# A linear recurrence's gate products: three rounded passes in place of plain fp32, in a planned one-core decoder kernel

## The chip, the cores and the metric

The kernel runs on one core of one Trainium2 chip. The metric is the device time of one execution in microseconds (us). Before the change three runs gave 982.98, 983.00 and 983.11 us, a median of 983.0.

## The reference, cut to what matters

One layer of a hybrid decoder: 512 tokens, model width 1024. Three token mixers read one input projection; their outputs are projected, multiplied by sigmoid gates, summed and projected again; cross-attention and a gated feed-forward network follow. The change lies in the first mixer, a gated linear recurrence over 512 channels in 4 blocks of 128:

```python
def rg_lru(u, w_a, b_a, w_i, b_i, lam):          # u: 512 tokens x 512 channels, after a causal conv
    ub = u.reshape(B_, L, LRU_BLOCKS, LRU_BLOCK)
    r = jax.nn.sigmoid(jnp.einsum('blhi,hij->blhj', ub, w_a).reshape(B_, L, BRANCH_W) + b_a)
    i = jax.nn.sigmoid(jnp.einsum('blhi,hij->blhj', ub, w_i).reshape(B_, L, BRANCH_W) + b_i)
    log_a = -LRU_C * r * jax.nn.softplus(-lam)
    a = jnp.exp(log_a)
    mult = jnp.sqrt(-jnp.expm1(2.0 * log_a))
    _, h = lax.associative_scan(_linear_combine, (a, mult * (i * u)), axis=1)
    return h
...
    y_a = rg_lru(causal_dwconv(u_lru, conv_w, conv_b), ...) * jax.nn.gelu(g_lru)
...
    merged = jnp.sum(gates * jnp.einsum('blnw,nwd->blnd', ys, w_branch), axis=2)
    return merged @ w_mix_out
```

The two einsums with `w_a` and `w_i` are the gate products: for each of 4 blocks and 2 kinds one product of a 128 x 128 weight and a 128 x 512 activation. The second mixer (GLA) is a chunked gated linear attention on q, k, v with a normalised output times silu(og). The third (S5) is a complex diagonal state-space model.

## The kernel before, in words

Activations lie with channels on 128 partitions and 512 tokens along the free axis, so most tiles are 128 x 512 floats. Almost every large product is done by `mm3`: both operands are split into a rounded high part (type fp32r, by a ScalarE Copy) and the rest (by a VectorE subtract), and three fp32r matmuls add high x high, high x low and low x high into one PSUM tile. The split of a weight is named `whi<-raw` (ScalarE, 128 x 1024) and `wlo<-raw,whi` (VectorE, 128 x 1024); that of a 128 x 512 activation is made by `hilo` (high part on ScalarE, low part on VectorE). The gate products `lg` of the recurrence are an exception: they are eight plain fp32 matmuls.

TensorE's stream has a foreground, written out in a fixed order: the projections us, u, g, qk (four tiles each), lr, v and og (tile `vo`), then for 24 output tiles a gate projection `gt` (24 matmuls) and a branch product `br` (12 matmuls), whose product with the gate is added up. The first eight `br` tiles read branch A, that is the recurrence's output `ya`, the next eight branch B (`yb`, GLA), the last eight branch C. Around it run background generators: `lru()` (the recurrence), `gla()` and the S5 routines. They are woven in by a planner. Each engine is wrapped by a class that adds up a guessed time for each instruction issued to it; at each `slot()` in the foreground a background generator may go on as long as VectorE and ScalarE are guessed to be less than a lead ahead of TensorE, and as long as what it waits for is guessed to be ready. The planner's guess for a matmul of n columns is n/2.4 + 13 ns in fp32r and n/0.6 + 26 ns in plain fp32. The guesses only set the order in which each engine's instructions are written; on the chip each engine runs its own list in that order, and waits at an instruction whose input or memory is not there.

Two pools of memory matter. All 128 x 512 SBUF tiles come from one heap of `NHEAP = 52` slots; a tile that is allocated into a slot may be written only when the last reader of the slot's earlier tile is through. PSUM tiles likewise take the slots of earlier PSUM tiles.

Names that are used below:

- `uc` is the conv's output, `lg` the gate products, `lgs` their sigmoids. `ea` and `th` come from an exponential and a tanh of them; three VectorE operations make a and 1-a^2 out of them; four ScalarE square roots (`ea<-ea`) give the factor of the input; then per block one VectorE product (`lgs<-lgs,ea`) and one VectorE scan (`ea<-th,lgs`), then the product with the GeLU gate (`ea<-ea,g`) and the split into `ya` high (ScalarE) and low (VectorE).
- In `gla()`: `keT` (transposes and copies), `dS` (state increments, 56 matmuls in two halves), `Sp` (14 VectorE steps that run the state over chunks), `att`, `o`, then for each of four token tiles `ob`: four ScalarE squares that sum into `ms`, a POOL power, four VectorE products; at the end `ybT`, transposes of the four `ob`.
- In S5: `Et` (transposes) and `G` (products), `E`, `C`, `tm` (VectorE products for tables), `es`, `esw`, `vv`, `zs` (its scan), `Xs`, `y`.
- `vo` on VectorE adds a bias, and on ScalarE is the silu of og. `th<-gt` and `th<-th,br` finish a gate and multiply it by its branch tile.

In the profile almost every instruction carries line 75 (the wrapper's `return f(*a, **k)`), so rows are told apart by tile names.

Of the kernel before, what the change touches and what calls it, by code (L numbers as in the profile page):

```python
# [16 lines left out]
P = 128  # L17
# [141 lines left out]
def hybrid_kernel(ctx: ExitStack, tc: tile.TileContext, I, out, dbg=None):  # L159
# [17 lines left out]
    def H(s, dt=F32):  # L177
        t = heap.tile([P, 512], dt, tag="h", name=nm(s))
        plan.life[t.name] = [plan.seq, plan.seq, nslot[0]]
        return t  # L180
# [10 lines left out]
    def PS(s):  # L191
        return psp.tile([P, 512], F32, tag="ps", name=nm(s))
# [3 lines left out]
    T, SP = Engine(nc.tensor, pe_cost, plan), Engine(nc.sync, sp_cost, plan)  # L196

    def split(hi, lo, src):
        A.activation(hi, src, AF.Copy)
        V.tensor_tensor(lo, src, hi.bitcast(F32), ALU.subtract)  # L200

    def hilo(s, src):
        hi, lo = H(s, F32R), H(s, F32R)
        split(hi, lo, src)
        return hi, lo

    def tap(name, ap, idx=None):
        if dbg is not None and name in dbg:
            d = dbg[name] if idx is None else dbg[name][idx]
            SP.dma_start(d, ap)  # L210
# [157 lines left out]
    def hold(n):  # L368

        while held[0] + n > NHOLD and not rush[0]:  # L370
            yield -1
        held[0] += n
# [31 lines left out]
    def note(x):  # L404
        LOG.append((nslot[0], x))
# [34 lines left out]
    def mm3(ps, w, x, first, last, **k):  # L440
        T.matmul(ps, lhsT=w[0], rhs=x[0], start=first, stop=False, **k)
        T.matmul(ps, lhsT=w[0], rhs=x[1], start=False, stop=False, **k)
        T.matmul(ps, lhsT=w[1], rhs=x[0], start=False, stop=last, **k)

    def cut(pair, *idx):
        return pair[0][idx], pair[1][idx]

    ALL = slice(None)
# [27 lines left out]
    def col(name, i=0, n=1):  # L476
        c = COLS[name] + i
        return pc[:, c:c + n]
# [108 lines left out]
    for f in range(8):  # L587
# [3 lines left out]
        o = ps[:, (f % 2) * 256:(f % 2) * 256 + 256]  # L591
# [28 lines left out]
    def lru_sp():  # L620
        lam = col("lam", 0, 4)
        t0, t1, t2, z, z2, acc = (S("sp", 4) for _ in range(6))
        V.tensor_scalar(t0, lam, -1.0, None, ALU.mult)
        V.tensor_tensor(t1, lam, t0, ALU.max)
        A.activation(t1, t1, AF.Exp, scale=-1.0)
        V.tensor_scalar(t2, t1, 2.0, None, ALU.add)
        V.reciprocal(t2, t2)
        V.tensor_tensor(z, t1, t2, ALU.mult)
        V.tensor_tensor(z2, z, z, ALU.mult)
        V.memset(acc, 1.0 / 17.0)  # L630
        for n in (15, 13, 11, 9, 7, 5, 3, 1):
            V.tensor_tensor(acc, acc, z2, ALU.mult)
            V.tensor_scalar(acc, acc, 1.0 / n, None, ALU.add)
        V.tensor_tensor(acc, acc, z, ALU.mult)
        V.tensor_scalar(t0, t0, 0.0, None, ALU.max)
        V.scalar_tensor_tensor(t0, acc, 2.0, t0, ALU.mult, ALU.add)
        V.tensor_scalar(lrsp[:, 0:4], t0, -8.0, None, ALU.mult)
        V.tensor_scalar(lrsp[:, 4:8], t0, 4.0, None, ALU.mult)
        yield 0
# [3 lines left out]

    def lru():
        yield from lru_sp()
        uc = []
        wa = [H("wa"), H("wi")]
        SP.dma_start(wa[0], I["lru_wa"])
        SP.dma_start(wa[1], I["lru_wi"])
        for b in range(4):  # L650
            o = H("uc")
            V.tensor_scalar(o, ug[b], col("cw", 12 + b), col("cb", b), ALU.mult, ALU.add)
            yield 0
            for s in range(1, 4):
                V.scalar_tensor_tensor(o[:, s:], ug[b][:, :SEQ - s], col("cw", 4 * (3 - s) + b), o[:, s:],
                                       ALU.mult, ALU.add)
                yield 0
            uc.append(o)
        ug.clear()
        yield T, uc[0], wa[0], wa[1]  # L660
        r, iu = [], []
        for b in range(4):
            yield from hold(2)
            pss = [PS("lg"), PS("lg")]
            for kind in range(2):
                T.matmul(pss[kind], lhsT=wa[kind][:, b * P:(b + 1) * P], rhs=uc[b], start=True, stop=True)
            yield A, pss[0], pss[1]
            for kind in range(2):
                o = H("lgs")
                A.activation(o, pss[kind], AF.Sigmoid, bias=col("bi" if kind else "ba", b))  # L670
                (iu if kind else r).append(o)
            held[0] -= 2
            yield 0
        for b in range(4):
            V.tensor_tensor(iu[b], iu[b], uc[b], ALU.mult)
        uc.clear()
        yield 0
        a, m = [], []
        for b in range(4):
            ea, th = H("ea"), H("th")  # L680
            A.activation(ea, r[b], AF.Exp, scale=lrsp[:, b:b + 1])
            A.activation(th, r[b], AF.Tanh, scale=lrsp[:, 4 + b:5 + b])
            yield V, ea, th
            V.scalar_tensor_tensor(th, ea, 1.0, th, ALU.add, ALU.mult)
            V.scalar_tensor_tensor(ea, th, 2.0, th, ALU.subtract, ALU.mult)
            V.tensor_scalar(th, th, -1.0, 1.0, ALU.mult, ALU.add)
            a.append(th)
            m.append(ea)
            yield 0
        r.clear()  # L690
        for b in range(4):
            A.activation(m[b], m[b], AF.Sqrt, scale=-1.0)
        lru_done.append(True)
        for b in range(4):
            yield V, m[b]
            V.tensor_tensor(iu[b], iu[b], m[b], ALU.mult)
            V.tensor_tensor_scan(m[b], a[b], iu[b], 0.0, ALU.mult, ALU.add)
            tap("lru_h", m[b], b)
            yield 0
        while len(gg) < 4:  # L700
            yield -1
        for b in range(4):
            V.tensor_tensor(m[b], m[b], gg[b], ALU.mult)
            tap("ya", m[b], b)
            ya[b] = hilo("ya", m[b])
            yield 0
        gg.clear()
        note("lru done")
# [524 lines left out]
    for f in range(4):  # L1233
# [3 lines left out]
        o = H("us")  # L1237
# [6 lines left out]
    for f in range(4):  # L1244
# [3 lines left out]
        o = H("u")  # L1248
        A.activation(o, ps, AF.Identity, bias=col("u", f))
        ug.append(o)  # L1250
        slot()
    e_lru = start_bg(lru(), True)
    for f in range(4):
        w = take("w_g")
        ps = PS("g")
        wstat(ps, w, h0T)
        o = H("g")
# [3 lines left out]
    for f in range(4):  # L1261
# [3 lines left out]
        o = H("qk")  # L1265
# [8 lines left out]
    for k in range(KD):  # L1274
        for j in range(2):
            T.matmul(ps[0:32, :], lhsT=w[:, 32 * k:32 * k + 32], rhs=h0T[k][j],
                     start=k == 0 and j == 0, stop=k == KD - 1 and j == 1)
    o = H("lr")
# [609 lines left out]
```

## Time and profile before

| what | value |
|---|---|
| median of three runs | 983.0 us (982.98 to 983.11) |
| the profiled execution | 983.31 us, of which the profiled span is 981.6 and 1.7 lie around it |
| TensorE busy in the span | 968.7 us (99%), 5552 instructions |
| VectorE, ScalarE, POOL busy | 633.4 us (65%), 419.9 us (43%), 184.7 us (19%) |
| share of TensorE in the chain that ended last | 96% |

The profiled execution is 0.3 us above the median. A busy share is a mean over the whole span; whether an engine waits somewhere is read from windows of the span, and what it waits for from the order of its instructions.

### The profile page before, as it was taken

How to read it: one execution, taken by the hardware profiler on the slowest of the kernel's cores; microseconds unless marked ns; L12 is line 12 of the kernel's file. 1: busy time of each engine (PE TensorE's matmuls, PEld its weight loads, DVE VectorE, ACT ScalarE, POOL GpSimd, SP SyncE). 2: the span in 40 equal slices, each digit the busy share in tenths (PEclk: the TensorE clock that was granted, in tenths of full speed). 3: DMA queues.
4: the chain of work that ended last, by engine and by line, in shares of the span. 5: the costliest groups of instructions: out<-in, count | busy, mean ns of one | idle time of the engine just before them, and what ended most of it. 6: DMA issues, size and time to landing. Idle time of an engine off the chain costs nothing.

```text
span 981.6 us, 14137 instructions
## 1 busy us (share of the span) xinstructions
PE 968.7 (99%) x5552; PEld 836.8 (85%) x5552; DVE 633.4 (65%) x981; ACT 419.9 (43%) x674; POOL 184.7 (19%) x281
## 2 busy tenths in 40 slices
PE   8999999999999999999999999999999999999996
PEld 7788777878888888888888888999999999988885
DVE  5724897798477563556684645885887787852317
ACT  5644366533224323543363433553545445542301
POOL 1389970042512301012000000200000000200001
PEclk9999999999999999999999999999999999999999
DMA  9942233233434454447142312342323332733202
GB/s 350 345 141 92 86 91 107 96 109 94 122 108 171 129 161 154 147 132 255 44 151 86 108 56 74 108 145 70 108 87 108 117 113 94 273 117 104 89 19 86
DMA packets 43554, 123.85 MB, mean 126 GB/s; under 512 B 5440, under 2 KB 5856, under 8 KB 43488
## 3 DMA queue, kind: packets, MB, share of 16 engines
q1 hardware_dynamic: 35040, 97.79, 29.1%
q0 software_dynamic: 6592, 22.02, 6.9%
q10 hardware_dynamic: 1856, 3.15, 1.2%
q8 instruction: 43, 0.70, 0.3%
q14 instruction: 23, 0.19, 0.1%
HBM read 109.31 MB, written 11.53 MB: 123 GB/s over the span
## 4 chain that ended last, share of the span: by engine, by line
PE 96%; DMA 2%; DVE 1%; SPq 0%; ACT 0%; issue 0%; POOL 0%; POOLq 0%; DVEq 0%
PE p L75 21%; PE gt L75 14%; PE wb L75 11%; PE br L75 7%; PE wc L75 5%; PE xq L75 5%; PE vo L75 4%; PE wa L75 3%; PE f L75 2%; PE qk L75 2%; PE us L75 2%; PE xv L75 2%; PE g L75 2%; PE u L75 2%; DMA raw<-in_w_xk 1%; PE y L75 1%
## 5 line engine op out<-in xcount | busy, mean ns | idle before, releaser
L75 DVE TENSOR_TENSOR wlo<-raw,whi 128x1024 fp32r<-128x1024 f32 x162 | 197.5, 1234 | 78.0 <-PE p L75 43.3
L75 ACT ACTIVATE whi<-raw 128x1024 fp32r<-128x1024 f32 x162 | 169.9, 1058 | 113.1 <-PE p L75 36.3
L75 PE MATMUL p<-whi,act 128*128 128x512 f32 x352 | 108.6, 389 | 0.0
L75 PE MATMUL gt<-h0Th,whi 128*128 128x512 f32 x192 | 79.2, 413 | 0.0
L75 PEld LDWEIGHTS p<-whi,act 128*128 128x128 f32 x352 | 66.1, 188 | 13.6
L75 PE MATMUL gt<-h0Th,wlo 128*128 128x512 f32 x192 | 75.0, 391 | 0.0
L75 PE MATMUL gt<-h0Tl,whi 128*128 128x512 f32 x192 | 74.9, 390 | 0.0
L75 PE MATMUL p<-wlo,act 128*128 128x512 f32 x176 | 68.5, 389 | 0.0
L75 POOL TENSOR_TENSOR st<-st,mh 128x1 f32<-128x1 f32 x16 | 15.3, 956 | 268.5 <-DVE st L75 262.8
L75 PE MATMUL wb<-h2Th,wlo 128*128 128x256 f32 x216 | 61.1, 283 | 0.0
L75 PE MATMUL wb<-h2Tl,whi 128*128 128x256 f32 x216 | 61.1, 283 | 0.0
L75 PE MATMUL wb<-h2Th,whi 128*128 128x256 f32 x216 | 61.1, 283 | 0.0
L75 ACT ACTIVATE th<-gt,gbh 128x512 f32<-128x512 f32 x24 | 16.6, 691 | 98.4 <-PE gt L75 89.4
L75 POOL DMA_DIRECT2D lnp<-in_lnp x12 | 6.5, 548 | 247.8 <-issue 197.6
L75 PE MATMUL wc<-s,whi 128*128 128x256 f32 x288 | 52.6, 283 | 0.0
L75 ACT ACTIVATE whi<-t 128x1024 fp32r<-128x1024 f32 x27 | 27.7, 1054 | 40.3 <-DVE t L75 35.9
L75 PEld LDWEIGHTS wc<-s,whi 128*128 128x128 f32 x288 | 44.9, 192 | 0.0
L75 PEld LDWEIGHTS gt<-h0Th,wlo 128*128 128x128 f32 x192 | 36.1, 188 | 7.7
L75 PEld LDWEIGHTS wb<-h2Tl,whi 128*128 128x128 f32 x216 | 41.5, 192 | 0.0
L75 PEld LDWEIGHTS wb<-h2Th,whi 128*128 128x128 f32 x216 | 41.5, 192 | 0.0
L75 PEld LDWEIGHTS wb<-h2Th,wlo 128*128 128x128 f32 x216 | 41.5, 192 | 0.0
L75 PEld LDWEIGHTS gt<-h0Th,whi 128*128 128x128 f32 x192 | 36.2, 189 | 5.8 <-issue 0.2
(393 smaller groups left out, 2512.0 us busy)
## 6 DMA issues: line engine op xcount, KB each, us to landing
raw<-in_w_gu SPq DMA_DIRECT2D x72, 256.0 KB, 2.9
raw<-in_w_dn SPq DMA_DIRECT2D x22, 512.0 KB, 3.6
raw<-in_w_xk SPq DMA_DIRECT2D x8, 512.0 KB, 6.8
raw<-in_w_gatea SPq DMA_DIRECT2D x8, 512.0 KB, 3.4
raw<-in_w_gateb SPq DMA_DIRECT2D x8, 512.0 KB, 3.5
raw<-in_w_gatec SPq DMA_DIRECT2D x8, 512.0 KB, 4.4
raw<-in_w_xv SPq DMA_DIRECT2D x8, 512.0 KB, 3.5
raw<-in_w_mix SPq DMA_DIRECT2D x8, 512.0 KB, 3.7
```

What stands on the lines that cost most here:

```text
L75: return f(*a, **k)
```

## The change

`lru()` splits the two gate weights and each conv output with `hilo`, once each, and forms the gate products with `mm3`. So 8 fp32 matmuls become 24 fp32r matmuls, and 6 ScalarE Copies and 6 VectorE subtracts of 128 x 512 are added. Twelve more heap tiles are taken (`wah`, `wih`: two each; `uch`: eight); `uch` is let go after the gate loop. No DMA is added, and the order on SyncE, which issues the loads, is the same. The loops that run are otherwise the same, but since the planner's guesses differ, it writes background work in other places from the recurrence on; from the S5 output product (`glu`) on, the order is again as before.

```diff
     def lru():
         yield from lru_sp()
-        uc = []
+        uc, uch = [], []
         wa = [H("wa"), H("wi")]
...
             uc.append(o)
+            if b == 0:
+                wa = [hilo("wah", wa[0]), hilo("wih", wa[1])]
+            uch.append(hilo("uch", o))
         ug.clear()
-        yield T, uc[0], wa[0], wa[1]
+        yield (T, *uch[0], *wa[0], *wa[1])
         r, iu = [], []
         for b in range(4):
             yield from hold(2)
             pss = [PS("lg"), PS("lg")]
             for kind in range(2):
-                T.matmul(pss[kind], lhsT=wa[kind][:, b * P:(b + 1) * P], rhs=uc[b], start=True, stop=True)
+                mm3(pss[kind], cut(wa[kind], ALL, slice(b * P, (b + 1) * P)), uch[b], True, True)
             yield A, pss[0], pss[1]
...
             held[0] -= 2
             yield 0
+        uch.clear()
         for b in range(4):
             V.tensor_tensor(iu[b], iu[b], uc[b], ALU.mult)
         uc.clear()
```

**ScalarE: where the four square roots stand.** Before, at the end of the recurrence's exponentials, ahead of the GLA's (`ax`); the numbers in names are the order of allocation.

```order
L75 ACTIVATE ea_1443<-lgs_1228,lrsp 128x512
L75 ACTIVATE th_1444<-lgs_1228,lrsp 128x512
L75 ACT_TABLE_LOAD
L75 ACTIVATE ea_1236<-ea_1236 128x512
L75 ACTIVATE ea_1286<-ea_1286 128x512
L75 ACTIVATE ea_1330<-ea_1330 128x512
L75 ACTIVATE ea_1443<-ea_1443 128x512
L75 ACTIVATE whi_1456<-raw_1380 128x1024
L75 ACTIVATE ax_1484<-xf_1436,pc 128x512
```

With the change, on the same engine, behind all of the GLA's exponentials, the four silus (the last is the first row here) and the copies of `keT`:

```order
L75 ACTIVATE vo_1730<-vo_1730 128x512
L75 ACTIVATE keT_1743<-keT_1733 128x512
L75 ACTIVATE keT_1745<-keT_1734 128x512
L75 ACT_TABLE_LOAD
L75 ACTIVATE ea_1212<-ea_1212 128x512
L75 ACTIVATE ea_1460<-ea_1460 128x512
L75 ACTIVATE ea_1641<-ea_1641 128x512
L75 ACTIVATE ea_1683<-ea_1683 128x512
L75 ACTIVATE whi_1756<-raw_1654 128x1024
L75 ACT_TABLE_LOAD
L75 ACTIVATE th_1785<-gt_1760,gbh 128x512
```

The roots have moved from ahead of the GLA's exponentials to behind the silu of og, and a weight split (`whi_1756`) stands behind them.

**VectorE: what stands between the bias adds of og and the state steps.** Before, two weight splits and the four blocks of `ya`; the products and scans (`lgs<-lgs,ea`, `ea<-th,lgs`) are all ahead of the first row here.

```order
L75 TENSOR_TENSOR vo_1705<-vo_1544,bvo_1539 128x512 [waits PE_49]
L75 TENSOR_TENSOR wlo_1708<-raw_1584,whi_1668 128x1024 [waits DMAHW3_49,Activation_49]
L75 TENSOR_TENSOR ea_1236<-ea_1236,g_878 128x512
L75 TENSOR_TENSOR ya_1757<-ea_1236,ya_1756 128x512 [waits Activation_49]
L75 TENSOR_TENSOR wlo_1760<-raw_1626,whi_1710 128x1024 [waits DMAHW4_49]
L75 TENSOR_TENSOR ea_1286<-ea_1286,g_946 128x512
L75 TENSOR_TENSOR ya_1795<-ea_1286,ya_1794 128x512 [waits DMASW2_49,Activation_49]
```

With the change, from the last bias add on:

```order
L75 TENSOR_TENSOR vo_1730<-vo_1556,bvo_1551 128x512 [waits PE_49]
L75 SCALAR_TENSOR_TENSOR th_1684<-ea_1683,th_1684 128x512 [waits Activation_49]
L75 SCALAR_TENSOR_TENSOR ea_1683<-th_1684 128x512 [waits DVE_49]
L75 TENSOR_SCALAR th_1684<-th_1684 128x512 [waits DVE_49]
L75 TENSOR_TENSOR wlo_1754<-raw_1610,whi_1693 128x1024 [waits DMAHW3_49,Activation_49]
L75 TENSOR_TENSOR wlo_1787<-raw_1654,whi_1756 128x1024 [waits DMAHW4_49,Activation_49]
L75 MEMSET Sp_1820 128x128
L75 MEMSET Sp_1822 128x128 [waits PE_49]
L75 TENSOR_TENSOR lgs_1170<-lgs_1170,ea_1212 128x512
L75 SCALAR_TENSOR_TENSOR ea_1212<-th_1213,lgs_1170 128x512 [waits DVE_49]
```

Behind the last row come three more such pairs, and only then the four blocks of `ya`. `wlo_1787` needs `whi_1756`, so VectorE's list from there on stands behind the square roots.

**ScalarE: the squares of the second token tile (`ob`), in the GLA's output stage.** Before, the squares wait for VectorE and for a DMA, and for no matmul:

```order
L75 ACTIVATE th_2132<-gt_2103,gbh 128x512 [waits DVE_49,PE_49]
L75 ACTIVATE ob_2139,ms_2138<-o_2034 128x128 [waits DMASW1_49,DVE_49]
L75 ACTIVATE ob_2139,ms_2138<-o_2035 128x128 [waits DVE_49]
L75 ACTIVATE ob_2139,ms_2138<-o_2034 128x128
L75 ACTIVATE ob_2139,ms_2138<-o_2035 128x128
L75 ACTIVATE es_2147<-e_2069 128x512 [waits Activation_49]
```

With the change:

```order
L75 ACTIVATE th_2232<-gt_2207,gbh 128x512 [waits DVE_49,PE_49]
L75 ACTIVATE ob_2239,ms_2238<-o_2097 128x128 [waits PE_49]
L75 ACTIVATE ob_2239,ms_2238<-o_2098 128x128
L75 ACTIVATE ob_2239,ms_2238<-o_2097 128x128
L75 ACTIVATE ob_2239,ms_2238<-o_2098 128x128
L75 ACTIVATE whi_2274<-raw_2184 128x1024 [waits DMAHW6_49]
```

The tile `ob_2239` has another slot of the heap, and the wait on TensorE that its first square now has is for the last reader of that slot's earlier tile, `en_1588` (the keys times the inverse decay): the next token tiles' `att_2306`, which stands later on TensorE than the `o` that is squared.

## Rows read from the trace of the kernel before

**Rows 1.** The page's busy time by engine: us (share of the span) x instructions.
```profile
PE 968.7 (99%) x5552; PEld 836.8 (85%) x5552; DVE 633.4 (65%) x981; ACT 419.9 (43%) x674; POOL 184.7 (19%) x281
```

**Rows 2.** One window: its us, engines' busy us (instructions), TensorE's granted clock, DMA share, GB/s.
```profile
97.00:590.00 493.00, 493.00 (x2609) 408.42 (x2608) 326.78 (x502) 203.68 (x358) 112.92 (x150) 1.00 0.37 120
```

**Rows 3.** The chain that ended last, in order of time: start, us, engine and tile.
```profile
104.62 5.44 PE qk L75 x24
110.06 1.72 PE lg L75 x4
...
117.27 5.15 PE lg L75 x12
...
182.72 5.44 PE gt L75 x24
...
199.95 2.18 PE dS L75 x56
202.12 1.64 PE att L75 x16
203.76 1.02 PE Et L75 x8
...
205.51 2.99 PE br L75 x12
```

**Rows 4.** ScalarE in order of time: start, us, operation, tiles, [idle before <-releaser].
```profile
146.35 1.28 ACT L75 ACT_TABLE_LOAD   x1
147.64 2.19 ACT L75 ACTIVATE ea<-ea 128x512 f32<-128x512 f32 x4
149.74 1.04 ACT L75 ACTIVATE whi<-raw 128x1024 fp32r<-128x1024 f32 x1
...
183.20 2.43 ACT L75 ACTIVATE vo<-vo 128x512 f32<-128x512 f32 x4 [2.71 <-DVE vo L75]
...
188.79 1.07 ACT L75 ACTIVATE keT<-keT 128x512 f32<-128x512 f32 x2
```

**Rows 5.** VectorE in order of time, 161 to 207 us.
```profile
161.61 0.68 DVE L75 TENSOR_TENSOR lgs<-lgs,ea 128x512 f32<-128x512 f32 x1
...
163.47 0.67 DVE L75 TENSOR_TENSOR lgs<-lgs,ea 128x512 f32<-128x512 f32 x1
...
182.48 2.48 DVE L75 TENSOR_TENSOR vo<-vo,bvo 128x512 f32<-128x512 f32 x4
...
197.78 0.69 DVE L75 TENSOR_TENSOR ya<-ea,ya 128x512 fp32r<-128x512 f32 x1 [0.70 <-ACT ya L75]
198.39 0.69 DVE L75 TENSOR_TENSOR ea<-ea,g 128x512 f32<-128x512 f32 x1
199.78 0.69 DVE L75 TENSOR_TENSOR ya<-ea,ya 128x512 fp32r<-128x512 f32 x1 [0.70 <-ACT ya L75]
...
201.86 5.35 DVE L75 SCALAR_TENSOR_TENSOR Sp<-Sp,dec,dS 128x128 f32<-128x128 f32 x14
```

**Rows 6.** ScalarE in order of time: the first of four squares of a token tile.
```profile
258.81 0.27 ACT L75 ACTIVATE ob<-o 128x128 f32<-128x128 f32 x1
```

**Rows 7.** VectorE in order of time, 259 to 273 us.
```profile
259.98 0.17 DVE L75 TENSOR_SCALAR ms<-ms 128x4 f32<-128x4 f32 x1 [12.72 <-ACT ob L75]
...
265.87 1.22 DVE L75 TENSOR_TENSOR wlo<-raw,whi 128x1024 fp32r<-128x1024 f32 x1
267.00 0.68 DVE L75 TENSOR_TENSOR esw<-esw,phi 128x512 f32<-128x512 f32 x1
...
271.39 1.12 DVE L75 SCALAR_TENSOR_TENSOR ob<-o,ms,vo 128x128 f32<-128x128 f32 x4
```

**Rows 8.** Two windows at the end of the span, columns as in rows 2.
```profile
973.00:977.50 4.50, 0.46 (x3) 0.03 (x1) 3.51 (x13) 0.81 (x2) 0.92 (x1) 1.00 0.30 117
977.50:981.60 4.10, 0.00 (x0) 0.00 (x0) 1.09 (x2) 0.00 (x0) 0.00 (x0) 0.50 0.34 128
```

**Rows 9.** The chain that ended last, later: the end of the GLA stage.
```profile
278.50 1.75 PE ybT L75 x16
```

## The prediction, on record before the changed kernel was run

> **What bounds the kernel now.** I read the page first: TensorE is busy 99% of the span and no other engine over 65% [rows 1]. Then windows, since a mean can hide a stage with room: from 97 to 590 us TensorE is busy 493.00 us of 493.00 at granted clock 1.00 [rows 2], which is its upper level, 2.4 GHz. So the stretch that the change touches has no wait of TensorE in it to win back. Time can be saved there only by giving TensorE less to do, and any wait that a new order brings is added in full, since the engine has no slack to catch up. The third view is the chain that ended last, which gives what each piece costs TensorE [rows 3].
>
> **What the change takes from TensorE.** The eight plain products stand in the chain as 1.72 us (two) and 5.15 us (six), 6.87 together [rows 3]. A foreground group of 24 fp32r matmuls of the same 128 x 512 shape takes 5.44, or 0.227 each. The 24 new matmuls therefore take 5.44, and a few hundredths for changing between the two kinds go: I take 1.5 us saved (1.4 to 1.6).
>
> **What it adds elsewhere.** Six Copies and six subtracts of 128 x 512. A subtract of this shape takes 0.61 us of VectorE's line (198.39 minus 197.78, rows 5), so 3.7 us there, and less on ScalarE. They stand ahead of the gate products, which in the new order run after qk's third tile, 10 us later than the first of them before. By then the operands are there, and TensorE has the qk tiles to do meanwhile. I cost the splits themselves at nothing, 0.6 us if the last subtract is late.
>
> **What it moves.** This is the larger part. The four square roots go from ahead of the GLA's exponentials to behind the silu of og, and the recurrence's products and scans go with them, on a VectorE list that itself waits at `wlo_1787` for a split that stands behind the roots. I walk through the new lists with durations of the rows, in times of the old trace less 1.5 us.
>
> *First wait.* TensorE ends og at 182.7 - 1.5 = 181.2. It then has keT (0.9: what is left of the 14.0 us from 188.16 to `att` at 202.12 after two gates of 5.44 and `dS`), three gates of 5.44, and half of `dS` (1.1), and comes to the first branch product at 199.5. That needs 12 x 0.227 = 2.7 us and would end at 202.2 [rows 3]. ScalarE: the last bias add ends 0.9 after og's last matmul, at 182.1 (an estimate from one add of about 0.6 and the passage), the last silu 0.65 later as before (185.63 against 182.48 + 2.48), so 182.75; the copies of keT take 1.0, the table load 1.3 (146.35 to 147.64), the four roots 2.15, the weight's high part 1.0 [rows 4, 5]: 188.2. VectorE: `wlo_1787` 1.2 (189.4); two memsets, 0.3 (what remains between `ya` at 199.78 plus 0.61 plus a weight's low part of 1.13 and `Sp` at 201.86, rows 5 and 7); then four pairs of product and scan at 1.86 each (163.47 minus 161.61), 7.4: 197.1. Then four blocks of `ya` at 2.0 each (199.78 minus 197.78), the last one done at 205.2 [rows 5]. The branch product takes the blocks in this order, so two matmuls remain after the last, and it ends at 205.7: **3.5 us of waiting**.
>
> *Second wait.* Behind the last `ya` VectorE has two low parts (2.3), one product with the branch tile (0.6) and `Sp`, of which TensorE's `G` waits for the sixth step (it takes the PSUM slot that these steps read): 6 x 5.35/14 = 2.3. That is 210.4. TensorE has half of `dS`, `att` 1.64 and `Et` 1.0, and is there at 209.5 [rows 3, 5, 7]: **0.9 us**.
>
> *Third wait.* The squares of `ob_2239` wait for the last reader of their heap slot in the second `att`. Call the end of that `att` T. On TensorE follow `Et` (1.0) and `G`, and `G` needs the PSUM slot of a branch tile, which is read by the product `th_2027`. On VectorE that product stands behind the `ms` of those squares. From the first square to `ms` 1.17 pass (258.81 to 259.98), then 0.1, and from `esw` through the scan to the end of such a product 4.4 (267.00 to 271.39) [rows 6, 7]. With 0.3 for the two passages between engines `G` starts at T + 6.0 in place of T + 1.2: **4.8 us**. Right behind it the second `y` matmul waits for `Xs`: after the product VectorE has the four `ob` (1.05), a low part (1.13), two `att` copies and two products (0.6 each), about 4.7, against `G`, one branch product and three gate matmuls, 4.4: **0.3 us**.
>
> *Fourth wait.* `ybT` needs the fourth `ob`. VectorE first waits for the first branch product after the second `o`, then has in its list ten products for S5's next tables and three around the bias (13 x 0.61), two low parts (2.3), three products with branch tiles (1.8), one `ob` (1.05), and the squares between (1.2): 14.5 us to the first part of the last `ob`. TensorE has behind that same branch product two more (5.4), four `e` (0.2 to 0.25 each) and a gate (5.44), about 12: **2.5 us**. Before, `ob` is done at 272.5 and `ybT` starts at 278.50, 6.0 us of cover [rows 7, 9].
>
> From there on I find no wait: the lists come together, and what TensorE lost is not regained, since its work stays the same.
>
> **The sum.** -1.5 + 3.5 + 0.9 + 4.8 + 0.3 + 2.5 = +10.5 us. On the profiled execution's 983.3 this is 993.8, on the median of 983.0 it is 993.5. I predict 994. Bounds for the unseen: each wait can be nothing if VectorE gets through earlier than the rows say (981.8 in all), and the third may be 1 us longer if the weights' low parts get in its way.
>
> One price can be checked against a page. The load of a ScalarE table costs 1.3 us in the line, from its own start to the first root, with no idle behind it [rows 4]. The Trainium skill, "ScalarE: Activation LUTs", section "What ACT_TABLE_LOAD costs", gives 1.28 us and a drain of 1.38 us besides, 2.66 for a switch. By that (an estimate) the roots would end 1.4 us later, and the sum would be 995.2. The row shows no such drain, so I stay with it.
>
> **Rivals.**
>
> *The new order costs nothing.* Then only the 1.5 us remain: 981.8, within 0.2% (2.0 us, about what a measurement of this kernel can tell from no change). It is decided at one place above all: whether `ya`'s last block is there by 201.7. For it speaks that VectorE has some idle time there, 0.70 us in each block of `ya` shown [rows 5], which a low part of a weight would fill anyway; against it that the chain silu, roots, split, scans, `ya` is serial, and 3.5 us too long for each of its rows at its measured duration. Chance 0.12.
>
> *Only the first two waits.* If a slot comes free earlier than I read from the lists, the third and fourth waits are covered, as in the kernel before, where `ob` has 6.0 us to spare [rows 7, 9]: 983.3 - 1.5 + 4.4 = 986.2, range 985 to 988. Chance 0.2.
>
> *The clock falls in the third wait.* After the last matmul, which ends at 973.46, the granted clock stays 1.00 until 977.5 and is 0.50, the lower level of 1.2 GHz, from there on [rows 8]. So 4.0 us of an idle TensorE were enough at that place, and the third wait is 4.8. How long the lower level would then last no row shows; if as long as the wait that brought it, 4.8 us of time hold half of the work, 2.4 us are lost: 996.2, range 995.5 to 998. The Trainium skill, "TensorE: Matmul & The Clock Gate", section "HAM oscillation — how this bites in real kernels", says that idle gaps in a matmul stream send the array back to half its clock, and that this is paid at each gap; the trace shows the fall at its end, but no such gap within. Chance 0.17.
>
> **How the numbers follow.** My forecast, 988 to 995.5, has 0.45; the three rivals 0.12, 0.2 and 0.17; 0.03 each are left for more than 998 and for faster by over 0.2% (under 981.0). The range from 985 to 998 leaves out 0.18. Slower by over 0.2%: 0.85; within: 0.12; faster: 0.03.
>
> **What the profile after would show.** The `lg` tile: 24 matmuls at 0.227 spacing between the third and fourth qk tile. ScalarE: a table load and four roots about 2 us behind the silu of og. TensorE: an idle of 3 to 4 us in front of or within the first branch product, released by VectorE's `ya`; one of about 1 before the first `G` (by `Sp`); one of about 5 before the second `G`, released by `th`; 2 to 3 within `ybT`, released by `ob`. A granted clock under 1.00 in the window behind the second `G` would show the third rival. I am wrong if TensorE is busy throughout from 97 to 300 us, or if there are waits at other places, in the S5 part after 280 us above all, where I looked at the lists with less care.

## The result, and the profile after

The changed kernel takes 999.9 us (median of four runs, 996.06 to 1001.64) against 983.0: 1.6% slower, ratio 1.0162 with an interval of 1.0148 to 1.0176. I had forecast 994 with a range to 998. The direction and three of the four places were right; the loss is 17 us where I had 11.

The profiled execution took 998.6 us, with a span of 996.9, 15.3 more than before. The waits of TensorE, 97 to 420 us (engine, tile, releaser; us in total, times, the longest):

```profile
PE G L75 <- DVE th L75: 4.6, 1, 4.6
PE ybT L75 <- DVE ob L75: 2.2, 1, 2.2
PE br L75 <- ACT ya L75: 1.1, 2, 0.5
PE br L75 <- DVE ya L75: 0.5, 2, 0.2
```

Before there was none [rows 2]. Three of the four predicted places are there, with the predicted releasers (at the first ScalarE's half of `ya` is one too); the second, `G` behind `Sp`, is missing. The branch product, the chain's first large loss, in order of time on TensorE:

```profile
200.75 0.62 PE L75 MATMUL br<-ya,whi 128*128 128x512 f32 x2
201.20 0.39 PE L75 MATMUL br<-ya,wlo 128*128 128x512 f32 x1
201.43 1.01 PE L75 MATMUL br<-ya,whi 128*128 128x512 f32 x2
202.28 0.39 PE L75 MATMUL br<-ya,wlo 128*128 128x512 f32 x1
203.20 0.49 PE L75 MATMUL br<-ya,whi 128*128 128x512 f32 x1 [0.54 <-ACT ya L75]
203.93 0.50 PE L75 MATMUL br<-ya,whi 128*128 128x512 f32 x1 [0.23 <-DVE ya L75]
204.26 0.40 PE L75 MATMUL br<-ya,wlo 128*128 128x512 f32 x1
205.19 0.50 PE L75 MATMUL br<-ya,whi 128*128 128x512 f32 x1 [0.53 <-ACT ya L75]
205.92 0.50 PE L75 MATMUL br<-ya,whi 128*128 128x512 f32 x1 [0.23 <-DVE ya L75]
206.26 0.40 PE L75 MATMUL br<-ya,wlo 128*128 128x512 f32 x1
```

Its twelve matmuls take from 200.75 to 206.6, 5.85 us, against 2.72 without waiting: 3.1 lost in small pieces, since the blocks of `ya` come 2.0 apart. The waits view counts 1.6 of them, because it takes the pipelined matmul before a wait as still busy. ScalarE and VectorE in order of time show the chain behind it:

```profile
183.46 1.07 ACT L75 ACTIVATE keT<-keT 128x512 f32<-128x512 f32 x2
184.53 1.28 ACT L75 ACT_TABLE_LOAD   x1
185.83 2.19 ACT L75 ACTIVATE ea<-ea 128x512 f32<-128x512 f32 x4
187.93 1.04 ACT L75 ACTIVATE whi<-raw 128x1024 fp32r<-128x1024 f32 x1
```
```profile
189.00 1.23 DVE L75 TENSOR_TENSOR wlo<-raw,whi 128x1024 fp32r<-128x1024 f32 x1 [3.19 <-ACT whi L75]
...
197.75 0.67 DVE L75 TENSOR_TENSOR ea<-ea,g 128x512 f32<-128x512 f32 x1
...
205.17 0.69 DVE L75 TENSOR_TENSOR ya<-ea,ya 128x512 fp32r<-128x512 f32 x1 [0.70 <-ACT ya L75]
```

The last `ya` starts at 205.17 and ends 0.69 later, at 205.86; I had it done at 205.2. But this trace stands 1.0 later from its beginning on (below), so VectorE was 0.3 earlier than I had it, and TensorE, which comes to the branch product at 200.75, 0.3 later than my 199.5. So the walk through the lists was good to a few tenths here.

The third wait begins on ScalarE, whose first square of the second token tile stands until the second `att` is through:

```profile
254.25 0.28 ACT L75 ACTIVATE ob<-o 128x128 f32<-128x128 f32 x1 [6.96 <-PE att L75]
```

`Et` follows `att` on TensorE at 254.37, and `G` starts at 260.11, 5.74 later; I had 6.0. What the walk lacked is in the windows (us, busy us of TensorE, weight loads, VectorE, ScalarE, POOL, then TensorE's granted clock, DMA share, GB/s):

```profile
200.00:207.00 7.00, 5.36 (x25) 2.84 (x25) 4.83 (x8) 3.75 (x6) 1.39 (x2) 1.00 0.35 111
207.00:214.00 7.00, 7.00 (x62) 6.11 (x60) 6.51 (x17) 1.67 (x2) 0.00 (x0) 0.51 0.01 4
255.00:260.00 5.00, 0.46 (x5) 0.22 (x3) 4.33 (x9) 1.99 (x7) 1.63 (x1) 0.82 0.11 43
260.00:265.00 5.00, 4.89 (x41) 4.06 (x42) 4.97 (x12) 3.07 (x11) 1.55 (x2) 0.50 0.51 145
265.00:300.00 35.00, 32.80 (x192) 26.48 (x191) 17.65 (x32) 7.80 (x24) 15.37 (x15) 1.00 0.29 92
```

Behind both long waits TensorE is busy at half clock, 0.51 and 0.50, that is 1.2 GHz, for about 7 and 5 us. The chain shows what that does to single pieces:

```profile
206.65 2.04 PE dS L75 x28
208.69 3.02 PE att L75 x16
211.71 1.90 PE Et L75 x8
...
260.11 1.29 PE G L75 x30
261.40 4.67 PE br L75 x12
```

`att` took 1.64 and `Et` 1.02 before [rows 3]; a half of `dS` by itself takes 1.30 at the full clock (the run with the fillers, below).

### The profile page after: what moved, and what is told of

The parts are those of the page before. It is cut to its first block, busy times and chain, and to the rows that moved or that the text cites. A ratio compares the mean times of both kernels' runs of the same rounds, so it can differ in the third digit from the quotient of the medians.

```text
span 996.9 us, 14162 instructions
## 1 busy us (share of the span) xinstructions
PE 976.0 (98%) x5560; PEld 844.0 (85%) x5560; DVE 636.6 (64%) x987; ACT 425.0 (43%) x680; POOL 183.2 (18%) x281
## 4 chain that ended last, share of the span: by engine, by line
PE 91%; DVE 4%; DMA 2%; ACT 1%; issue 0%; SPq 0%; POOL 0%; POOLq 0%; DVEq 0%; ACTq 0%
PE p L75 21%; PE gt L75 11%; PE wb L75 10%; PE br L75 6%; PE wc L75 5%; PE xq L75 4%; PE vo L75 4%; PE wa L75 3%; PE f L75 2%; PE xv L75 2%; PE us L75 2%; PE g L75 2%; PE u L75 2%; PE qk L75 2%; DMA raw<-in_w_xk 1%; PE y L75 1%
## 5 line engine op out<-in xcount | busy, mean ns | idle before, releaser
L75 DVE SCALAR_TENSOR_TENSOR th<-th,br 128x512 f32<-128x512 f32 x24 | 16.4, 683 | 40.9 <-PE br L75 40.9
```

## The experiments

All times are medians, and each ratio is to runs of the kernel before on the same chip. It is taken over all runs, so it can differ a little from the quotient of the two medians (1.0172 for the result above).

**The arithmetic alone.** The splits and the 24 matmuls are issued without the planner's knowledge, and it books the old eight. All lists are those of before with the new instructions inserted:

```diff
-                mm3(pss[kind], cut(wa[kind], ...), uch[b], True, True)
+                T._account("matmul", (pss[kind],), dict(lhsT=wf[kind][...], rhs=uc[b], ...))
+                for j, (x, y) in enumerate(((0, 0), (0, 1), (1, 0))):
+                    nc.tensor.matmul(pss[kind], lhsT=w[x], rhs=uch[b][y], start=j == 0, stop=j == 2)
```

> The changed arithmetic in the old order: the splits and the 24 rounded matmuls are issued where the old kernel had its eight plain ones, and the planner books the old eight, so every engine's list is that of before with the new instructions inserted. Theory 'order' (the loss is made by where the planner writes the background work, not by the new products): 1.5 us less than before, 981.5 (981.0 to 982.3), with TensorE busy all through 97 to 590 us. Rival 'arithmetic' (splits, twelve more tiles or the 24 matmuls themselves make the waits): 990 or more, with waits of TensorE at the gate products or behind the branch products.

Measured: 982.8 against 983.7, ratio 0.9993 (0.9984 to 1.0002). No loss, and no gain that can be told from nothing. One wait of TensorE is left:

```profile
PE qk L75 <- ACT lgs L75: 0.7, 1, 0.7
```

Of the 1.5 us saved about half is given back there: a qk tile waits for the PSUM slot of `lg`, which the first sigmoid reads, and that stands on ScalarE behind the last conv block's Copy.

**The order alone.** The lists are those of the changed kernel, with splits and tiles, but eight plain products (the split parts are made and not used):

```diff
-                mm3(pss[kind], cut(wa[kind], ...), uch[b], True, True)
+                for j, (x, y) in enumerate(((0, 0), (0, 1), (1, 0))):
+                    T._account("matmul", (pss[kind],), dict(lhsT=w[x], rhs=uch[b][y], ...))
+                nc.tensor.matmul(pss[kind], lhsT=wf[kind][...], rhs=uc[b], start=True, stop=True)
```

> The converse: every list as in the changed kernel, splits made and tiles taken, but the gate products are again the eight plain fp32 matmuls (the split parts are made and not used). Theory 'order': as slow as the changed kernel and 1.5 us more, 1001.4, with the same spread from run to run (997 to 1003.5). Rival 'the three-pass products make the loss': back to 983 to 985.

Measured: 1002.2 (996.43 to 1003.55), ratio 1.0176 (1.0150 to 1.0202). The same waits of 4.6, 2.2 and 1.3 us. So the new products in the old order lose nothing, and the new order loses as much with the old products: the loss comes with the order. Both kernels make the splits and take the twelve tiles; what the new order would cost without them, no run shows.

**The clock.** 31 matmuls whose results nobody reads, ahead of the two long waits:

```diff
             ps = PS("br")
+            if n == "a" and f == 0:
+                for j in range(15):
+                    nc.tensor.matmul(ps, lhsT=h0T[j % 8][0][:, 0:P], rhs=h0T[j % 8][0], start=True, stop=True)
...
             pse = [PS("Et"), PS("Et")]
+            if q == 1:
+                for j in range(16):
+                    nc.tensor.matmul(pse[0], lhsT=h0T[j % 8][0][:, 0:P], rhs=h0T[j % 8][0], start=True, stop=True)
```

> The changed kernel with 31 extra matmuls whose results are overwritten and never read: 15 ahead of the first branch product (3.4 us) and 16 ahead of the transposes Et of the second S5 group (3.6 us), both in front of waits of TensorE. Theory 'clock' (about 6 us of the loss is work done at the lower clock behind the two long waits): granted clock 1.00 from 200 to 290 us, the rows of att and Et again at 1.64 and 1.02 us, 993.8 (992 to 995.5), and runs within 1 us of each other where those of the changed kernel spread over 5.6; the wait in front of G by Sp (0.9) comes back. Rival 'the slow rows come from something else, such as contention for memory': unchanged, 996 to 1002.

Measured: 994.5 (992.84 to 994.79), ratio 1.0106 (1.0092 to 1.0119). TensorE does more work and the kernel is 5.4 us faster than the changed one (4.2 in the profiled spans, of which 1.35 lies at the beginning, where the clock did not fall in this execution), with `att` and `Et` at their old durations and half of `dS` at 1.30 for 2.04:

```profile
205.68 1.30 PE dS L75 x28
206.99 1.64 PE att L75 x16
208.63 1.04 PE Et L75 x8
```

The granted clock is 1.00 from 200 to 290. I had said up to 290; behind the wait of `ybT`, which nothing fills, it is below:

```profile
290.00:300.00 10.00, 7.82 (x36) 6.59 (x35) 9.12 (x19) 5.36 (x9) 4.02 (x4) 0.83 0.55 157
```

The wait of `G` for `Sp` did not come back (expected 0.9); a wait of 0.9 for `th` is left at the second `G`, which starts 5.74 behind the end of `att` as in the changed kernel. The runs lie 2.0 us apart, where I had said within 1.

**The heap slot, first try.** The squares write to a tile of their own:

```diff
+    sq = const.tile([P, P], F32, name="sq")
...
-                    A.activation(o[:, h * P:(h + 1) * P], src, AF.Square, accum_out=ms[:, h:h + 1])
+                    A.activation(sq, src, AF.Square, accum_out=ms[:, h:h + 1])
```

> The changed kernel, but the squares of the GLA's output stage, of which only the sums are used, are written to a small tile of their own instead of the ob tile. Their heap slot is then first written by VectorE, behind th. Theory 'heap slot' (the 4.6 us wait of the second G begins at the slot that the squares wait for): that wait shrinks to about 1.6 us, since the scan zs still takes a slot that the same att frees; the second stretch at the lower clock goes too; 993 to 996. Rival 'VectorE is late there by itself': the wait and the time stay, 996 to 1002.

Measured: 999.8, ratio 1.0156 (1.0134 to 1.0179): nothing gained, expected 993 to 996. The wait had only moved, as VectorE and the waits view show:

```profile
253.68 1.13 DVE L75 SCALAR_TENSOR_TENSOR ob<-o,ms,vo 128x128 f32<-128x128 f32 x4 [8.87 <-PE att L75]
```
```profile
PE G L75 <- DVE th L75: 6.1, 1, 6.1
```

In this kernel the first `ob`, not the second, has the slot that `att` frees, and VectorE stands at it for 8.87 us with the rest of the list behind. The edit changed who takes which slot; it gave no more slots. So it doesn't tell the theories apart, and the next two were made.

**The heap slot, one and two slots more.** First the norm gain, which held a slot of 2 KB to the end of the stage for 512 bytes a partition, gets a tile of its own; then also the scan writes into its first operand:

```diff
-    SP.dma_start(glaw[:, 0:P], I["gla_g"].partition_broadcast(P))
+    ngc = const.tile([P, P], F32, name="ngc")
+    SP.dma_start(ngc, I["gla_g"].partition_broadcast(P))
...
-        zs = H("zs")
+        zs = es
```

> The changed kernel, but the GLA's norm gain (128 x 128, used until the end of that stage) lies in a small tile of its own, and its heap slot is free early: one more heap slot for the output stage, every list the same. Theory 'heap slot': the squares of the second token tile no longer wait for att, the scan zs does, so the second G waits about 1.7 us in place of 4.6, too short for the clock to fall: 994.5 (993 to 996.5). Rival 'VectorE is late there by itself': 996 to 1002.

> As the one-slot kernel, and the scan zs is written into the tile of its first operand, so that it takes no slot either. Theory 'heap slot': the wait of the second G is gone and so is the stretch at the lower clock behind it: 7.1 us less than the changed kernel, 992.8 (991 to 994.5). Rival: 996 to 1002.

Measured: 994.9 (994.56 to 995.79), ratio 1.0119 (1.0102 to 1.0136), and 992.7 (992.13 to 994.38), ratio 1.0099 (1.0084 to 1.0114). The wait of the second `G` goes from 4.6 to 1.4 with one slot:

```profile
PE G L75 <- DVE th L75: 1.4, 1, 1.4
```

where now the scan, as expected, stands at the slot that `att` frees:

```profile
254.42 1.23 DVE L75 TENSOR_TENSOR_SCAN zs<-es,vv 128x512 f32<-128x512 f32 x1 [5.13 <-PE att L75]
```

It goes to none with two, where from 250 to 270 the clock stays up:

```profile
250.00:270.00 20.00, 19.87 (x149) 16.55 (x148) 9.56 (x16) 6.07 (x15) 9.15 (x10) 1.00 0.42 135
```

With one slot the clock stayed at 1.00 behind the wait of 1.4 us too. That so short a wait never brings it down is not shown: behind one of 1.65 us at the beginning of the changed kernel's span it fell (below).

**The first wait.** One low part of a weight, on which VectorE waits behind the roots, is written behind `ya`:

```diff
-            w = take("w_gate" + n)
+            w = take("w_gate" + n, AHEAD - (n == "a" and f == 1))
```

> The changed kernel, but the weight's low part on VectorE that waits behind the square roots (wlo_1787) is written one step later, behind the blocks of ya; nothing else moves. Theory 'order': the products and scans begin with the first root, ya's last block is there before the branch product needs it, the first wait (3.1 us in the trace after) and with it the first stretch at the lower clock (3.3) go, and about 1.3 us of the wait of G for Sp come back: 994.8 (993 to 996.5). Rival 'ya is late by its own serial chain': only the 1.2 us of that one operation, 997 to 1001.

Measured: 992.0 (991.67 to 993.53), ratio 1.0092 (1.0076 to 1.0107), 7.9 us less than the changed kernel where I expected 5, and below my range. The branch product runs without a wait and the clock stays 1.00 behind it; the wait for `Sp` is 0.7, not 1.3. In the profiled spans, 996.9 and 990.0, the difference is 6.9: 3.1 and 3.3 less 0.7, and 1.3 at the beginning of the span, where `us` starts at 38.99 and in the changed kernel at 40.28 (below). The edit also moves one high part on ScalarE, from 190.87 to behind the copies of `ya`; ScalarE was idle for 2.06 us behind it, so it was not on this chain. The waits that are left:

```profile
PE G L75 <- DVE th L75: 4.6, 1, 4.6
PE ybT L75 <- DVE ob L75: 2.2, 1, 2.2
PE G L75 <- DVE Sp L75: 0.7, 1, 0.7
```

**Both.** The later low part and the two slots:

> The later low part and the two heap slots together. If the waits add up as read, what is left over the kernel before is the wait of G for Sp (1.3) and that of ybT (2.3), less the 1.5 us that TensorE saves: 985 to 988, with granted clock 1.00 from 97 to 590 us and runs within 1 us of each other. If the waits replace each other: 990 or more.

Measured: 988.8 (986.42 to 989.71), ratio 1.0052 (1.0037 to 1.0067): 0.8 above my range, and under the 990 of the rival. The profiled execution is the fastest, with the clock at 1.00 from 97 to 590 us and two waits:

```profile
PE ybT L75 <- DVE ob L75: 2.2, 1, 2.2
PE G L75 <- DVE Sp L75: 1.5, 1, 1.5
```
```profile
97.00:590.00 493.00, 489.26 (x2603) 407.52 (x2602) 330.52 (x508) 208.10 (x364) 112.16 (x150) 1.00 0.37 119
```

That execution took 986.4 us, 3.2 over the 983.2 of the kernel before on the same chip; 3.7 us of waiting less the 1.5 us saved would be 2.2, so 1.0 us is not accounted for. The other three took 988.7 to 989.7, with a mean granted clock over the span of 0.993 to 0.995 where it has 0.997. So the waits add up to within about 1 us in the one execution with a trace. The runs did not come within 1 us of each other, as I had expected; by their mean clocks the lower level still appears in the other three, but where in the span, no trace shows.

**A version that could beat both.** The arithmetic in the old order, with the two weights loaded and split before the recurrence begins:

```diff
     for f in range(4):
         w = take("w_u")
...
+        if f == 1:
+            for x in ("wa", "wi"):
+                wf.append(H(x))
+                nc.sync.dma_start(wf[-1], I["lru_" + x])
+    wa += [hilo_q("wah", wf[0]), hilo_q("wih", wf[1])]
     e_lru = start_bg(lru(), True)
```

> The changed arithmetic in the old order, as in the order-kept kernel, but the two gate weights are loaded earlier and split before the recurrence begins, where VectorE and ScalarE have idle time (VectorE 81 to 90 us), not between the convs. In the order-kept kernel TensorE waits 0.7 us at a qk tile, for a sigmoid that stands behind the last conv block's split on ScalarE, and VectorE comes to that split 4.7 us later than before. Theory 'the six splits cost only where they delay the last conv block': 1.35 us of VectorE's line less ahead of it, the wait of 0.7 goes, and the time is the whole 1.5 us under before: 981.5 (981 to 982). Rival 'the wait has another cause' : 0.7 to 0.9 under before, as the order-kept kernel.

Measured: 982.9 against 983.1, ratio 0.9996 (0.9987 to 1.0005). The expectation failed: 0.2 us are gained, with an interval from 1.3 under to 0.5 over, and the wait is still there, 0.8 us. The last conv block's Copy starts at 117.83 where it started at 117.56, so 1.35 us less of subtracts ahead of it did not bring it forward. Both halves of that can be read from the traces. VectorE's small operations ahead of the convs ended 0.7 us later in this run, for a reason that stays open. And in the order-kept kernel the two weights' subtracts had filled the time in which VectorE waits for the first conv block's Copy; without them it is idle there for 0.70 us.

## Why the prediction was right in its places and wrong in its size

| term | predicted | in the profile after |
|---|---|---|
| the gate products | -1.5 | -1.4 (24 matmuls at 0.227 for 6.87) |
| first wait, `br` for `ya` | 3.5 | 3.1 |
| second wait, `G` for `Sp` | 0.9 | 0 |
| third wait, `G` for `th` | 4.8 | 4.6 |
| `y` for `Xs` | 0.3 | 0 |
| fourth wait, `ybT` for `ob` | 2.5 | 2.2 |
| lower clock behind the first wait | 0 | 3.3 |
| lower clock behind the third | 0 (a rival: 2.4) | 2.5 |
| lower clock at the beginning, 33 to 36 us | 0 | 1.0 |
| sum | +10.5 | +15.3 |

**What held.** The mechanism of the waits: the loss comes with the order (first two experiments), through three of the places named. The waits sum to 9.9 us where I had 12.0. The heap as the cause of the third is shown by dose: 4.6, 1.4 and 0 us with none, one and two slots more. That the first comes from the one low part that stands behind the roots is shown by moving it. The fourth no run takes away; its cause rests on the lists and on its size.

**What failed** is the term for the lower clock. Behind the first wait the prediction put it at nothing and gave no reason; behind the third it kept it out of the sum, as a rival with a chance of 0.17 and a price of 2.4 us. The trace shows 3.3 and 2.5 us in their place, and 1.0 at the beginning. Without these 6.8 us the profiled execution's 998.6 would be 991.8 (an estimate), 2 under the 993.8 that I had for it: the clock alone carried the time out of the range.

I had looked at the one fall in the trace of before, behind 4.0 us without work [rows 8], and so at the longest wait only. Here it fell behind less: in the stretch 200 to 207 TensorE is busy for 5.36 us of 7.00, with no single idle of more than 0.54 listed, and from 207 to 214 the clock is 0.51. That the slow rows are the clock's doing, and not contention, the filler shows: with more matmuls the same rows are back at their durations, at a granted clock of 1.00. The window of 207 to 214 itself has a DMA share of 0.01, so there was next to no transfer to contend with.

That the rival's 2.4 us came so near to 2.5 is luck. It let the lower level last as long as the wait, 4.8 us, all of it with work; by the windows it lasted from about 258 to 265, with TensorE at work in the last 4.9 us. Nor has a fall one price: in the kernel with one slot more the clock fell inside the first wait (0.75 over 200 to 207, 0.52 over 207 to 214), which makes about 10 us at the lower level (an estimate) where the changed kernel's trace has about 7.

**A smaller term**, the second wait, was too large by itself, and the clock hid the rest of it:

```profile
208.65 5.27 DVE L75 SCALAR_TENSOR_TENSOR Sp<-Sp,dec,dS 128x128 f32<-128x128 f32 x14
```

The sixth step is done at 208.65 + 6 x 5.27/14 = 210.9. At the full clock TensorE would have come to `G` at 206.65 + 1.30 + 1.64 + 1.04 = 210.6, so 0.3 of the 0.9 us would be there (an estimate); half of `dS` takes 1.30, where I had 1.1, and VectorE was earlier. At half clock TensorE is there at 213.6, and nothing is left. The 0.7 and 1.5 us in the two kernels with the later low part are no measure of it, since that low part stands there between `ya` and `Sp` and adds 1.1 us. The wait for `Xs` was covered likewise, by a branch product of 4.67 us for 2.72. So the waits and the clock are not independent terms.

The clock also makes the spread. The four runs of the changed kernel have mean granted clocks over the span of 0.992, 0.989, 0.987 and 0.987 with 996.1, 998.6, 1001.2 and 1001.6 us. The one with 998.6 has the trace; where the slower two lost more is read from their mean clocks only. The profiled one has also 1.0 us at the beginning, where the projection `us` starts at 40.28 in place of 39.31. TensorE there is behind a wait of 1.65 us that the kernel before has too, and in this execution the clock falls behind it; that is not the change's, since nothing differs up to there:

```profile
31.36 1.25 PE L75 MATMUL tp<-ident,lh 128*128 128x128 f32 x8 [1.65 <-DVE h0Tl L75]
```
```profile
34.00:36.00 2.00, 2.00 (x11) 2.00 (x11) 2.00 (x4) 1.60 (x4) 0.00 (x0) 0.50 0.98 356
```

The Trainium skill, "TensorE: Matmul & The Clock Gate", section "HAM oscillation — how this bites in real kernels", says that a gap in the matmul stream puts the array back to half its clock and that each gap pays again: this trace agrees for the third wait, one gap of 4.6 us with 0.50 behind it. The first, with 0.51 behind it, is no single gap, and behind the 2.2 us of `ybT` the clock stayed at 1.00 in this trace. The price of a table load was rightly taken from the row: the load starts at 184.53 as the copy before it ends, and the first root at 185.83, so 1.30 us in all, where the Trainium skill, "ScalarE: Activation LUTs", section "What ACT_TABLE_LOAD costs", has 2.66 for a switch.

## What to carry to other kernels

In a kernel whose order is set by guessed costs, a change of arithmetic is first a change of order: read the new lists of every engine, and test the two apart by booking the old cost for the new instructions. Where TensorE is busy all the time, a wait of a few us, even in small pieces, can cost more than itself, since the work behind it may run at half clock; price both, and expect the runs to spread. A pool that is full turns a tile's allocation into a wait for whoever used the slot before; here one slot more took 3.2 us off a wait of 4.6, with every engine's list as it was.

## What the runs showed of the hardware that I had not expected

- The granted clock fell to 0.50 behind a stretch with no listed idle of more than 0.54 us at a time (TensorE busy 5.36 of 7.00 us), and behind single waits of 1.65 us (ahead of the transposes `tp`) and 2.2 us (`ybT`, with the filler), while in other executions the same waits left it at 1.00.
- Adding 31 useless matmuls, 7 us of TensorE's time, made the kernel 5.4 us faster by the medians.
